# One scheduling block around a whole encoder kernel, ordered on another timing model

## Chip, cores and metric

The kernel runs on one core of one Trainium2 chip. The metric is the device time of one execution in microseconds (us); of several runs the median counts. Kernel before: median 1623.04 us of 3 runs, 1622.1 to 1624.04.

## What is computed

The reference is an encoder trunk of two layers over 512 tokens of width 1024, in float32:

```python
for layer in range(DEPTH):                       # 2
    h = rmsnorm(x, attn_norm[layer])
    proj = h @ w_in[layer]                       # 1024 x 6144: ten parts
    (a_q, a_k, a_v, b_q, b_ff, b_fb, b_i, b_g, gate_a, gate_b) = split_columns(proj)
    y_a = diff_attention(a_q, a_k, a_v, cos, sin, ...) @ w_a[layer]     # 4 heads, 2 softmaxes each
    y_b = hgrn2_bidirectional(b_q, b_ff, b_fb, b_i, b_g, ...) @ w_b[layer]   # 4 heads, gated recurrence
    merged = jax.nn.sigmoid(gate_a) * y_a + jax.nn.sigmoid(gate_b) * y_b
    x = x + merged @ w_o[layer]
    h = rmsnorm(x, ffn_norm[layer])
    x = x + (jax.nn.silu(h @ w_gate[layer]) * (h @ w_up[layer])) @ w_down[layer]   # hidden 2816
return rmsnorm(x, final_norm)
```

## The kernel before

**Arithmetic.** Every large product is made of three matmuls in a rounded float32 format: an operand is split into a high part (a cast on ScalarE) and a low part (a subtraction on VectorE), and `mm3` (line 207) multiplies high by high, high by low and low by high into the same PSUM bank. Activations are kept split in `hh` and `hl`, tokens along the free dimension; weights come as 1 MB loads into two buffers `raw` (`wload`, line 188, all on SyncE's DMA queue, SP) and are split into three buffers each of `hi` and `lo` (`wsplit`, line 196). `project_fm` (line 212) takes 128 output columns at a time: one split, 24 matmuls into one of four banks `m`, and a function that empties the bank. `project_tm` (line 234) does the same with tokens on the partitions.

**Stages of a layer.** First the projections that the recurrence needs. Then the recurrence, `hgrn_head` (line 412), head by head: a long chain of small steps on VectorE and ScalarE, with short groups of TensorE matmuls between them: transposes `kt` (line 494), states `st` (501), six groups of scores `sc` (548), `nr` (586 and 587), outputs `po` (599) and a norm `hss`. Beside them TensorE has projections for later steps to do. Then attention (line 627): sixteen steps, each with scores `qk` (662, 665), a softmax on VectorE and ScalarE, transposes `wt` (712), and for each head a product with the values; beside it the rest of the gate projections and w_b. Then w_a (its inputs are `oah` and `oal`), w_o, and the FFN (from line 828): one stream of matmuls through w_gate, w_up and w_down without small groups. The last layer ends in the final norm and the output.

**What sets the order.** The kernel is traced as one straight program. The Tile framework then decides the order of the instructions of each engine: it plays the program on a timing simulation of the chip, and each time an engine can take an instruction, it gives it the ready one of the highest priority. Priority is the place in the traced program; what is traced under `urgent()` (`tc.high_priority`) goes first of all: weight loads, splits, and the emptying of banks. So TensorE's order comes from three things: what the simulation takes for ready at a time, the place in the program, and edges added by hand. `behind(a, b)` (line 94) is such an edge: `a` is issued after `b`, without a wait on the chip; `tc.issue_after` is the same for a whole passage. Once the order is decided, each engine runs its own list strictly as it is listed, and semaphores hold an instruction until its operands are there. Pools with `reuse_waits="tile"` take over the memory of a pool before tile by tile. GpSimd makes an identity, five masks and constants at the start and does nothing later.

The change touches the place where the pools are opened, lines 100 to 105.

Of the kernel before, what the change touches and what calls it, by code (L numbers as in the profile page):

```python
# [47 lines left out]
def kernel(  # L48
# [45 lines left out]
    def behind(ins, other):  # L94
# [2 lines left out]
                          mybir.DependencyInfo(mybir.DependencyClass.NoSync, mybir.DependencyReason.DATA),  # L97
                          reason="keep the tensor engine from waiting")

    cp = ctx.enter_context(tc.tile_pool(name="const", bufs=1))  # L100
    wp = ctx.enter_context(tc.tile_pool(name="wraw", bufs=2))
    hp = ctx.enter_context(tc.tile_pool(name="wsplit", bufs=3))
# [862 lines left out]
```

## Time and profile before

| | |
|---|---|
| median of 3 runs | 1623.04 us |
| the profiled execution's own time | 1622.27 us |
| its span, first to last instruction | 1620.5 us |
| granted TensorE clock, mean | 0.999 of full |
| TensorE matmuls in the records | 7473 |
| VectorE, ScalarE busy in the span | 1013.2 us, 773.2 us |
| HBM read | 139.23 MB |

The profile is of one execution. Its page gives each engine's busy time; the windows give the same for stretches of the span, which show the stages: recurrence and attention of the first layer lie in the first 400 us, its FFN in the next 400, and the second layer repeats this in 800 to 1200 and 1200 to the end. A wait in the profile is idle time of an engine just before an instruction, with the instruction that released it. Matmuls are pipelined and the profile models their ends, so TensorE can be recorded as busy without working at its full pace; the number of matmuls in a stretch shows the pace. "PEld" is the loading of weights into TensorE, "SPq" SyncE's DMA queue.

### The profile page before, as it was taken

The page shows a single profiled execution, that of the slowest core. Times are in us where ns is not written, and L with a number is a line of the kernel's source. Part 1 is how long each engine was busy: PE and PEld are TensorE (multiplying, and loading weights), DVE is VectorE, ACT ScalarE, POOL GpSimd, SP SyncE. Part 2 cuts the span into 40 slices and gives each one's busy share as a digit, 9 for nine tenths or more (in the row PEclk, how much of TensorE's full clock was granted, in tenths as well). Part 3 has the DMA queues.
Part 4 walks back from the last instruction along what each step waited for, and adds up shares of the span by engine and source line. Part 5 has one row for each costly group of instructions (what it writes and reads, how often), then busy time and mean ns, then how long its engine had stood idle before and what let it go on. Part 6 is the DMA issues. An engine that isn't in the chain of part 4 may idle for free.

```text
span 1620.5 us, 18760 instructions
## 1 busy us (share of the span) xinstructions
PE 1604.7 (99%) x7473; PEld 1324.6 (82%) x7473; DVE 1013.2 (63%) x1637; ACT 773.2 (48%) x1188; POOL 8.5 (1%) x21
## 2 busy tenths in 40 slices
PE   9999999999999999999999999999999999999998
PEld 7888888887888888888888888888878888888886
DVE  8888977877654444433468789788875444444224
ACT  4666666676433323322355667676754323233213
POOL 2000000000000000000000000000000000000000
PEclk9999999999999999999999999999999999999999
DMA  6212221221333222322322222122123233332321
GB/s 203 91 57 73 79 68 63 79 78 52 105 104 98 85 88 94 115 90 99 103 89 87 70 79 78 54 77 79 52 79 98 84 104 104 105 101 94 104 82 74
DMA packets 118071, 142.53 MB, mean 88 GB/s; under 512 B 3168, under 2 KB 100704, under 8 KB 117984
## 3 DMA queue, kind: packets, MB, share of 16 engines
q1 hardware_dynamic: 117696, 141.05, 26.8%
q8 instruction: 58, 0.95, 0.2%
q10 hardware_dynamic: 288, 0.30, 0.1%
q14 instruction: 29, 0.24, 0.0%
HBM read 139.23 MB, written 2.10 MB: 87 GB/s over the span
## 4 chain that ended last, share of the span: by engine, by line
PE 86%; DVE 9%; ACT 3%; issue 1%; DMA 0%; SPq 0%; DVEq 0%; ACTq 0%
PE m L210 25%; PE m L208 24%; PE m L209 24%; DVE fl L81 2%; DVE lo L81 2%; PE sc L548 2%; PE s L209 1%; PE s L210 1%; PE s L208 1%; PE qk L665 1%; DVE z L81 1%; PE wt L712 1%; PE po L599 1%; PE qk L662 1%; ACT hi L92 1%
## 5 line engine op out<-in xcount | busy, mean ns | idle before, releaser
L92 ACT CAST hi<-raw 128x1024 fp32r<-128x1024 f32 (+2 forms) x274 | 272.2, 995 | 616.2 <-PE m L209 483.6
L208 PE MATMUL m<-hh,hi 128*128 128x512 f32 x1216 | 475.1, 391 | 0.7 <-ACT hh L78 0.7
L210 PE MATMUL m<-hh,lo 128*128 128x512 f32 x1216 | 475.3, 391 | 0.0
L209 PE MATMUL m<-hl,hi 128*128 128x512 f32 x1216 | 474.8, 391 | 0.0
L81 DVE TENSOR_TENSOR lo<-raw,hi 128x1024 fp32r<-128x1024 f32 (+2 forms) x282 | 321.0, 1139 | 181.6 <-ACT hi L92 180.2
L208 PEld LDWEIGHTS m<-hh,hi 128*128 128x128 f32 x1216 | 228.3, 188 | 48.5 <-ACT hh L78 1.9
L210 PEld LDWEIGHTS m<-hh,lo 128*128 128x128 f32 x1216 | 228.3, 188 | 47.3 <-DVE lo L81 0.6
L209 PEld LDWEIGHTS m<-hl,hi 128*128 128x128 f32 x1216 | 228.4, 188 | 46.9
L81 DVE TENSOR_TENSOR gu<-m,rbc 128x512 f32<-128x512 f32 x88 | 60.9, 692 | 241.6 <-PE m L210 237.6
L208 PE MATMUL m<-hi,hh 128*128 128x512 f32 x256 | 101.4, 396 | 0.0
L210 PE MATMUL m<-hi,hl 128*128 128x512 f32 x256 | 100.9, 394 | 0.0
L209 PE MATMUL m<-lo,hh 128*128 128x512 f32 x256 | 100.9, 394 | 0.0
L78 ACT ACTIVATE fl<-fl 128x1024 f32<-128x1024 f32 (+1 forms) x56 | 48.5, 872 | 43.6 <-DVE fl L81 43.5
L208 PE MATMUL m<-gh,hi 128*128 128x512 f32 x176 | 68.5, 389 | 0.0
L209 PE MATMUL m<-gl,hi 128*128 128x512 f32 x176 | 68.5, 389 | 0.0
L210 PE MATMUL m<-gh,lo 128*128 128x512 f32 x176 | 68.5, 389 | 0.0
L210 PEld LDWEIGHTS m<-hi,hl 128*128 128x128 f32 x256 | 48.1, 188 | 9.6
L208 PEld LDWEIGHTS m<-hi,hh 128*128 128x128 f32 x256 | 48.2, 188 | 9.3
L209 PEld LDWEIGHTS m<-lo,hh 128*128 128x128 f32 x256 | 48.2, 188 | 9.3
L548 PEld LDWEIGHTS sc<-fl 128*128 128x128 f32 x384 | 49.1, 191 | 7.0 <-issue 2.3
L548 PE MATMUL sc<-fl 128*128 128x128 f32 x384 | 51.3, 276 | 1.8 <-DVE fl L81 1.7
L209 PE MATMUL m<-ml,hi 128*128 128x512 f32 x128 | 49.7, 391 | 0.0
(258 smaller groups left out, 2349.9 us busy)
## 6 DMA issues: line engine op xcount, KB each, us to landing
raw<-in_w_in_dram SPq DMA_DIRECT2D x46, 1024.0 KB, 5.0
raw<-in_w_gate_dram SPq DMA_DIRECT2D x22, 1024.0 KB, 5.1
raw<-in_w_up_dram SPq DMA_DIRECT2D x22, 1024.0 KB, 5.2
raw<-in_w_down_dram SPq DMA_DIRECT2D x19, 1024.0 KB, 4.7
raw<-in_w_o_dram SPq DMA_DIRECT2D x8, 1024.0 KB, 4.8
raw<-in_w_b_dram SPq DMA_DIRECT2D x4, 1024.0 KB, 4.8
raw<-in_w_a_dram SPq DMA_DIRECT2D x4, 1024.0 KB, 5.0
raw<-in_w_down_dram SPq DMA_DIRECT2D x4, 768.0 KB, 4.1
```

Source lines behind the costliest of these rows:

```text
L78: return ACT.activation(o, i, func, **kw)
L81: return DVE.tensor_tensor(o, a, b, op)
L92: return ACT.copy(hi, src), tt(lo, src, hi.bitcast(F32), ALU.subtract)
L208: PE.matmul(ps, lh, rh, start=start, stop=False)
L209: PE.matmul(ps, lh, rl, start=False, stop=False)
L210: PE.matmul(ps, ll, rh, start=False, stop=stop)
L548: mm = PE.matmul(ps[:, c], K[:, c], Q[:, c], start=True, stop=True)
L599: mm = PE.matmul(po[:, tok], a, b, start=i == 0, stop=i == len(terms) - 1)
L662: mm = PE.matmul(ps[c], q2[:, c, tok], ka[:, c, :], start=True, stop=False)
L665: PE.matmul(ps[c], q2[:, c, tok], kb[:, c, :], start=False, stop=True)
L712: tr = PE.transpose(pt[:, s * P:(s + 1) * P], w[:, 0, s * P:(s + 1) * P], ident)
```

## The change

One line is added ahead of the pools, so that everything traced after it, which is the whole program, lies in one block:

```diff
+    ctx.enter_context(tc.block(schedule_with_timeline_sim=True))
     cp = ctx.enter_context(tc.tile_pool(name="const", bufs=1))
     wp = ctx.enter_context(tc.tile_pool(name="wraw", bufs=2))
     hp = ctx.enter_context(tc.tile_pool(name="wsplit", bufs=3))
```

`tc.block` traces its body into a basic block of its own, which is entered unconditionally and scheduled as a unit. With `schedule_with_timeline_sim=True` the framework orders that block on the second of its two timing simulations, which models the machine in more detail; the framework's own text names one thing that the first leaves out, a fixed cost of GpSimd's elementwise instructions. Everything else stays as it was: the traced instructions, their priorities, the edges added by hand, tiles, pools and buffer counts.

## The prediction

> **What bounds the kernel now.** I read the page first, then busy time by stage, then TensorE's waits, then its groups by shape.
>
> ```profile
> span 1620.5 us, 18760 instructions
> PE 1604.7 (99%) x7473; PEld 1324.6 (82%) x7473; DVE 1013.2 (63%) x1637; ACT 773.2 (48%) x1188; POOL 8.5 (1%) x21
> PE 86%; DVE 9%; ACT 3%; issue 1%; DMA 0%; SPq 0%; DVEq 0%; ACTq 0%
> ```
>
> TensorE (PE) is busy nearly throughout and makes up 86% of the chain that ended last. The windows show whether it is also fed at its own pace (columns: window, length, then busy time and count of PE, weight loads, VectorE, ScalarE, GpSimd, the clock, DMA):
>
> ```profile
> 0.00:50.00 50.00, 47.88 (x201) 38.10 (x202) 37.93 (x116) 27.51 (x38) 8.47 (x21) 1.00 0.52 175
> 50.00:100.00 50.00, 48.36 (x245) 40.25 (x244) 47.08 (x86) 27.88 (x43) 0.00 (x0) 1.00 0.26 84
> 150.00:200.00 50.00, 48.94 (x260) 41.08 (x259) 46.41 (x88) 29.76 (x53) 0.00 (x0) 1.00 0.26 85
> 350.00:400.00 50.00, 48.53 (x218) 38.23 (x217) 35.60 (x63) 32.17 (x60) 0.00 (x0) 1.00 0.13 43
> 600.00:650.00 50.00, 50.00 (x222) 41.39 (x221) 23.27 (x28) 14.79 (x18) 0.00 (x0) 1.00 0.28 86
> 950.00:1000.00 50.00, 49.37 (x257) 41.22 (x256) 48.92 (x89) 30.36 (x48) 0.00 (x0) 1.00 0.26 85
> 1150.00:1200.00 50.00, 48.55 (x219) 38.28 (x218) 35.66 (x64) 32.89 (x61) 0.00 (x0) 1.00 0.13 43
> sum 1650.00, PE 1604.71 PEld 1324.58 DVE 1013.20 ACT 773.18 POOL 8.47; mean PE 48.63 PEld 40.14 DVE 30.70 ACT 23.43 POOL 0.26
> ```
>
> Window 600 to 650 lies in the FFN: 222 matmuls of 512 columns in 50 us, no idle, 225.2 ns each. That is PE's pace when fed. The other six windows lie in the start, in the recurrence and at the two ends of attention, and there PE is idle for 2.1 + 1.6 + 1.1 + 1.5 + 0.6 + 1.5 = 8.4 us. The waits of PE name the same places (us in total, times, longest):
>
> ```profile
> PE m L210 <- DVE lo L81: 1.8, 2, 0.9
> PE sc L548 <- DVE fl L81: 1.7, 3, 1.1
> PE idle L266 <- DVE ones_r L119: 1.4, 1, 1.4
> PE st L501 <- ACT kt L496: 1.2, 1, 1.2
> PE m L208 <- ACT oah L92: 1.2, 2, 0.6
> PE m L208 <- ACT hh L78: 0.7, 1, 0.7
> PE nr L587 <- DVE kl L81: 0.3, 1, 0.3
> PE kt L494 <- ACT fs L78: 0.2, 1, 0.2
> PE qk L665 <- DVE kb L81: 0.2, 1, 0.2
> ```
>
> They sum to 8.7 us, 1.4 of it the very start. The records can hide more, since a matmul's end is modelled. So I count the work itself, by PE's groups (last columns: busy us and mean ns, then the idle before them):
>
> ```profile
> L548 PE MATMUL sc<-fl 128*128 128x128 f32 x384 | 51.3, 276 | 1.8 <-DVE fl L81 1.7
> L665 PE MATMUL qk<-kb,q 128*128 128x512 f32 x64 | 26.0, 406 | 0.5 <-DVE kb L81 0.2
> L712 PE MATMUL wt<-ident,e 128*128 128x128 f32 x128 | 19.2, 273 | 0.0
> L599 PE MATMUL po<-fs,S 128*128 128x128 f32 x96 | 15.9, 275 | 0.0
> L599 PE MATMUL po<-A,vB 128*128 128x128 f32 x64 | 12.5, 277 | 0.0
> L501 PE MATMUL st<-vB,kt 128*128 128x128 f32 x96 | 12.4, 279 | 1.2 <-ACT kt L496 1.2
> L494 PE MATMUL kt<-ident,fs 128*128 128x128 f32 x48 | 7.0, 275 | 0.2 <-ACT fs L78 0.2
> L638 PE MATMUL qkt<-ident,ak 128*128 128x128 f32 x32 | 4.8, 273 | 0.0
> L638 PE MATMUL qkt<-ident,aq 128*128 128x128 f32 x32 | 4.8, 272 | 0.0
> L884 PE MATMUL xt<-ident,xT 128*128 128x128 f32 x32 | 3.9, 276 | 0.1
> L210 PE MATMUL m<-oah,lo 128*128 128x512 f32 x64 | 24.6, 394 | 1.8 <-DVE lo L81 1.8
> L208 PE MATMUL m<-oah,hi 128*128 128x512 f32 x64 | 24.6, 394 | 1.2 <-ACT oah L92 1.2
> ```
>
> ```profile
> 227.58 2.02 PE po L599 x18
> 1487.50 2.53 issue
> ```
>
> Of the narrow ones, 384 + 128 + 96 + 64 + 96 + 48 + 3 x 32 = 912 have 128 columns, and eighteen of them in a row take 2.02 us, 112 ns each. So 912 x 0.112 + 6561 x 0.2252 = 102.1 + 1477.5 = 1579.7 us of matmuls, if nothing ever waited. The end lies behind them:
>
> ```profile
> 1613.78 0.28 PE L210 MATMUL s<-hi,gl 128*128 128x256 f32 x1
> 1616.99 0.35 ACTq L927 DMA_DIRECT2D out_dram<-xt  x1
> ```
>
> 1620.5 - 1614.1 = 6.4 us of tail and 1.4 us of start stand outside. What order could still give back inside is at most 1620.5 - 1579.7 - 6.4 - 1.4 = 33 us, of which 7.3 show as waits.
>
> [...] The page shows the weight loads busy for 82% of the span. [...]
>
> **The change part by part.** No arithmetic, operand, transfer or tile is added or removed. Three things change.
>
> *Which order each engine's instructions get.* Where PE has one stream of work only, there is nothing to reorder: I cost the FFN windows at 0, covered by the packed row 600 to 650. Where recurrence or attention is mixed with projections, PE switches between project_fm's matmuls (24 to a tile of 128 columns, 24 x 0.2252 = 5.4 us) and small groups that wait for VectorE or ScalarE. Those groups, from the rows above (records by records in one group): sc 384 / 8 = 48, st 96 / 6 = 16, kt 48 / 3 = 16, qk 64 / 2 = 32, wt 128 / 4 = 32, po 8 (one a head), 152 in all. Today the waits name 3 + 1 + 1 + 1 = 6 of them (sc, st, kt, qk), 3.3 us, 0.55 us a wait. The other 146 arrive after their operands. A new order is made from times of a model; how well they fit, no row shows. Bounds: below, all waits inside go and as much again of the hidden loss (-15 us); above, all 152 wait 0.55 us (+84 - 3 = +80). I take the value by the place. A late operand can't be made up where VectorE has no idle time: it is busy 47.1, 46.4 and 48.9 of 50 us in three windows, and at the two ends of attention, PE already waits for w_a's operands with the filler matmuls used up. That is five of the sixteen windows of 50 us in 0 to 400 and 800 to 1200, so 152 x 5 / 16 = 48 groups, x 0.55 = 26 us, less the 3.3 there now: **+23 us**.
>
> *What else moves with it.* The weight splits are traced at top priority and stay early in any order, but their exact place decides when the raw buffers come free:
>
> ```profile
> L81 DVE TENSOR_TENSOR lo<-raw,hi 128x1024 fp32r<-128x1024 f32 (+2 forms) x282 | 321.0, 1139 | 181.6 <-ACT hi L92 180.2
> SPq L193 <- DVE lo L81: 1432.3, 123, 38.3
> raw<-in_w_gate_dram SPq DMA_DIRECT2D x22, 1024.0 KB, 5.1
> ```
>
> SP's queue always waits for that split, then a load lands in 5.1 us and feeds 48 matmuls, 10.8 us. A split 1.1 us later moves the load by 1.1 us inside 5.7 us of cover: 0, and in FFN the same. If the cover went, the 123 waiting loads would each show what is over.
>
> *The block itself.* Each engine enters and leaves a block of instructions of its own. No row shows such a branch. Bounds: 0 (a fall-through; a gain is excluded, nothing is left out for it), and for one stall the longest time on the chain in which an engine waited for nothing that the profile shows, 2.53 us at 1487.5, where ScalarE reloads its table. Once at each end makes 5.1 us. I take 0, since the first loads come from SP at once in the same program, and keep 5 for the range.
>
> [...]
>
> The profiled execution took 1622.27 us, its span and 1.8 us around it; 1622.3 + 23 = 1645. The median of the runs is 0.8 us higher than that execution, so I round to 1646 us.
>
> **The rivals.**
>
> *The new order fits better (faster).* The model counts what the first one leaves out, so each small group is placed where its operands have landed. For it: the 6 waits of the small groups are such misfits, and projections stand ready to fill them. Against it: 33 us is all there is, and the 1.8 + 1.2 = 3.0 us before w_a's matmuls (rows m<-oah) at the attention ends have no filler. Time: 1622.3 less 7.3 - 3.0 = 4.3 shown and the same to twice that of hidden loss, -9 to -13: 1609 to 1614, I say 1612. It decides if fewer than those 6 groups wait.
>
> *Engines are filled ahead (much slower).* If the model lets PE take several ready matmuls before a small group becomes ready, every hand-off queues behind half a projection tile, 2.7 us. Attention makes 32 qk and 32 wt hand-offs, in series within a head: 64 x 2.7 = 173 us of longer chain, hidden as long as projections are left to run. They are used up by the end of attention today (rows m<-oah, windows 350 to 400 and 1150 to 1200), so part shows; a quarter to a half, 43 to 86 us: 1665 to 1708, I say 1685. For it: PE at 99% shows that it nearly always has other work ready. Against it: the manual edges (behind) hold some projections back.
>
> *Nothing moves that matters.* The order comes out nearly the same, because priorities, manual edges and buffer counts leave little choice, or since the models differ mainly for GpSimd, which works 8.47 us, all in the first window. 1623, within 3. Against it: 152 groups are placed by time.
>
> **How the numbers follow.** Forecast (small misfits) 0.31, its own range 1628 to 1665; filled ahead 0.23; fits better 0.28; no difference 0.18. A difference under 0.2% (3.2 us) is about what a measurement here can't tell from none. Slower: 0.31 + 0.23 = 0.54; same 0.18; faster 0.28. The range: below 1609 lies some 0.07 of the better-fit case, above 1692 about 0.11 of filled ahead, so 1609 to 1692.
>
> **What would show it.** Right: the count of each group unchanged, FFN windows still 222 matmuls in 50 us, PE idle grown in the windows with VectorE above 46 us and at the ends of attention, with sc, st, qk and oah named in PE's waits at about 0.5 us each and a few dozen times. Filled ahead: projections of gates finished early, then long stretches in attention with PE well under 48 of 50. Fits better: PE's waits inside under 4 us. Wrong altogether: a loss inside FFN, at the first load, or a grown tail.

## The result and the profile after

The changed kernel takes 1764.64 us (median of 4 runs, 1763.42 to 1766.52). The kernel before takes 1622.57 us (4 runs, 1622.08 to 1624.04). The ratio is 1.0876, its 95% interval 1.0864 to 1.0889: 142 us slower. The forecast was 1646 us with a range up to 1692. Its sign held; its size did not, and neither did the mechanism that it took for the likeliest.

The profiled execution after took 1766.52 us. From its page: span, engines, the chain that ended last, and TensorE's busy share and granted clock in 40 slices of 44 us.

```profile
span 1764.8 us, 18744 instructions
PE 1652.9 (94%) x7473; PEld 1362.2 (77%) x7473; DVE 1022.1 (58%) x1637; ACT 775.7 (44%) x1188; POOL 8.6 (0%) x21
PE 88%; DVE 7%; ACT 4%; issue 1%; DVEq 0%; ACTq 0%
PE   9998896996899999999999987879968999999998
PEclk9998996998899999999999999989989999999999
```

The work is the same, 7473 matmuls, but the span is 144 us longer, and the slices under 9 lie in two stretches, slices 4 to 11 and 24 to 31: the recurrence and attention of the two layers (slice 40 holds the tail). The windows of the kernel after, with the columns as in the prediction, say when inside them:

```profile
50.00:100.00 50.00, 50.00 (x243) 42.06 (x242) 40.20 (x72) 26.56 (x42) 0.00 (x0) 1.00 0.32 105
100.00:150.00 50.00, 50.00 (x257) 42.44 (x256) 38.60 (x65) 25.82 (x38) 0.00 (x0) 1.00 0.23 74
150.00:200.00 50.00, 38.79 (x179) 32.91 (x178) 37.14 (x73) 25.55 (x42) 0.00 (x0) 0.80 0.03 12
250.00:300.00 50.00, 33.29 (x145) 27.60 (x143) 28.28 (x57) 19.31 (x32) 0.00 (x0) 0.69 0.07 21
400.00:450.00 50.00, 33.68 (x129) 22.24 (x127) 36.88 (x72) 27.72 (x62) 0.00 (x0) 0.86 0.00 0
600.00:650.00 50.00, 50.00 (x223) 41.40 (x222) 22.90 (x28) 14.71 (x18) 0.00 (x0) 1.00 0.27 85
```

Read the first two rows beside the third. From 50 to 100 us TensorE is fuller than it was before (50.00 of 50 where 48.36 stood), while VectorE does less (40.20 where 47.08 stood) and the weight loads run ahead (105 GB/s where 84 stood). It stays full to 150 us. Then TensorE stands still: 11.2 us in 150 to 200, 16.7 us in 250 to 300, 16.3 us in 400 to 450, and hardly any weights are loaded there (DMA share 0.03, 0.07 and 0.00). What TensorE gained early it did not have later. The FFN row, 223 matmuls in 50 us, is as before (222).

The waits of TensorE after, the first rows (us in total, times, longest):

```profile
PE sc L549 <- DVE fl L81: 25.0, 11, 3.7
PE m L209 <- DVE avl L84: 13.6, 2, 6.8
PE m L209 <- ACT oah L92: 11.7, 6, 2.9
PE hss L405 <- ACT sqh L398: 11.6, 9, 1.3
PE m L209 <- DVE sg L81: 8.1, 2, 6.9
```

All such rows together sum to 105 us, against 8.7 before: 96 us more. The other 48 us of the longer span are in TensorE's busy time (1652.9 against 1604.7 for the same matmuls). Part of that is the clock, shown further down.

**Where it starts.** The first head of the recurrence, from the timelines (start, length, instruction, count, idle time before it). Before:

```profile
77.09 1.06 PE L548 MATMUL sc<-fl 128*128 128x128 f32 x8
...
80.74 1.06 PE L548 MATMUL sc<-fl 128*128 128x128 f32 x8
...
83.94 1.06 PE L548 MATMUL sc<-fl 128*128 128x128 f32 x8
...
88.04 1.06 PE L548 MATMUL sc<-fl 128*128 128x128 f32 x8
```

After:

```profile
79.68 1.06 PE L549 MATMUL sc<-fl 128*128 128x128 f32 x8
...
86.73 1.05 PE L549 MATMUL sc<-fl 128*128 128x128 f32 x8
...
93.55 1.05 PE L549 MATMUL sc<-fl 128*128 128x128 f32 x8
...
101.50 1.06 PE L549 MATMUL sc<-fl 128*128 128x128 f32 x8
```

The same groups came 3.65, 3.20 and 4.10 us apart and now come 7.05, 6.82 and 7.95 us apart, and TensorE does not idle between them. The timelines say what lies between the six groups: 12, 10, 14, 14 and 5 matmuls of projections before, 27, 26, 31, 29 and 19 after. For the first three gaps that is 15, 16 and 17 more; at 0.2265 us, the spacing of projections in these timelines, 3.40, 3.62 and 3.85 us. The gaps grew by 3.40, 3.62 and 3.85 us. So the whole stretching of these gaps is projections put ahead of a group that has to wait for them in TensorE's list. VectorE's timeline after shows that the groups' operands were there:

```profile
84.39 0.69 DVE L81 TENSOR_TENSOR fl<-fl,q 128x512 f32<-128x512 f32 x1
87.82 0.42 DVE L81 TENSOR_TENSOR fl<-cum 128x256 f32<-128x256 f32 x1 [2.74 <-PE sc L549]
...
90.38 0.69 DVE L81 TENSOR_TENSOR fl<-fl,q 128x512 f32<-128x512 f32 x1
```

The first row ends the operand `fl` of the group at 93.55, 8.5 us ahead of it, the last row that of the group at 101.50, 10.4 us ahead; before, the same two groups came 0.7 and 1.6 us after theirs. The middle row shows how the delay is handed on: VectorE starts the next `fl` only when the group at 86.73 has released a buffer.

How far this carries: the norm `hss` closes a head. The tile's rows, first and last start of the four heads, before (layer 1's recurrence, then attention in layers 1 and 2):

```profile
L404 PE MATMUL hss<-sqh,ones_r x4: 404/404/404, 107.4 to 233.3; 128*128 128x512 f32 x4
...
L407 PE MATMUL hss<-sql,ones_r x4: 389/402/424, 299.9 to 384.9; 128*128 128x512 f32 x4
...
L407 PE MATMUL hss<-sql,ones_r x4: 389/398/431, 1100.8 to 1185.8; 128*128 128x512 f32 x4
```

and after:

```profile
L405 PE MATMUL hss<-sqh,ones_r x4: 398/451/499, 140.4 to 285.4; 128*128 128x512 f32 x4
...
L408 PE MATMUL hss<-sql,ones_r x4: 389/398/503, 375.4 to 455.3; 128*128 128x512 f32 x4
...
L408 PE MATMUL hss<-sql,ones_r x4: 389/398/503, 1248.9 to 1329.3; 128*128 128x512 f32 x4
```

In layer 1 the first head of the recurrence ends 33 us later, the fourth 52 us later, attention 70 us later. When attention of layer 2 ends, 143.5 us are lost, nearly all of the 144 us of the longer span: 73 us of it in layer 2. About three quarters of layer 1's 70 us were there at the end of the recurrence.

### The profile page after: what moved, and what is told of

Same layout as the page of the kernel before. It is cut to its first block, busy times and chain, and to the rows that moved or that the text cites. A ratio compares the mean times of both kernels' runs of the same rounds, so it can differ in the third digit from the quotient of the medians.

```text
span 1764.8 us, 18744 instructions
## 1 busy us (share of the span) xinstructions
PE 1652.9 (94%) x7473; PEld 1362.2 (77%) x7473; DVE 1022.1 (58%) x1637; ACT 775.7 (44%) x1188; POOL 8.6 (0%) x21
## 4 chain that ended last, share of the span: by engine, by line
PE 88%; DVE 7%; ACT 4%; issue 1%; DVEq 0%; ACTq 0%
PE m L209 26%; PE m L210 26%; PE m L211 25%; PE sc L549 2%; DVE fl L81 2%; PE s L211 1%; PE s L210 1%; PE s L209 1%; PE po L600 1%; ACT hsq L78 1%; ACT fl L78 1%; ACT e L78 1%; PE qk L666 1%; PE qk L663 1%; PE wt L713 0%
## 5 line engine op out<-in xcount | busy, mean ns | idle before, releaser
L549 PE MATMUL sc<-fl 128*128 128x128 f32 x384 | 61.6, 314 | 25.7 <-DVE fl L81 25.0
L549 PEld LDWEIGHTS sc<-fl 128*128 128x128 f32 x384 | 57.3, 223 | 30.8 <-DVE fl L81 17.1
L211 PEld LDWEIGHTS m<-hi,hl 128*128 128x128 f32 x256 | 49.2, 192 | 10.4
L78 ACT ACTIVATE e<-qk,nm 128x512 f32<-128x512 f32 x64 | 43.8, 687 | 18.9 <-DVE nm L668 18.8
```

Source lines behind the costliest of these rows:

```text
L78: return ACT.activation(o, i, func, **kw)
L211: PE.matmul(ps, ll, rh, start=False, stop=stop)
L549: mm = PE.matmul(ps[:, c], K[:, c], Q[:, c], start=True, stop=True)
```

## The experiments

Three theories were stated. The first (T1): the second simulation lets TensorE take instructions well ahead of the time at which they run, so a group that becomes ready lands behind projections already taken; projections are used up early, and the chain then runs with nothing beside it. The second (T2): the same, but on VectorE and ScalarE. The third (T3): it is the times of the second model that put groups in wrong places. A rival without any order is the block itself. The second simulation has a setting for each engine, how many instructions it may hold ahead while the order is made; the kernel after has the simulation's own, 35 for TensorE and 12 for VectorE and ScalarE. They are settings of a model: how many instructions the chip's engines hold ahead, no trace here shows. The kernels below change that setting; the chip, the work and the edges stay. In the cuts of code each statement has a line of its own, and "..." marks what is left out. The runs of the kernel before that stand beside the experiments have a median of 1622.26 us.

**The block without the second simulation** (block_only).

```diff
-    ctx.enter_context(tc.block(schedule_with_timeline_sim=True))
+    ctx.enter_context(tc.block())
```

> The block stays, the second simulation goes (tc.block() without the argument). If the order from the second simulation is the cause, this runs as the kernel before: 1619 to 1627 us. If it is the block (its entry and exit, or that it is scheduled as a unit), it stays near 1765.

Measured: 1622.05 us, ratio 0.9998 (0.9989 to 1.0008). Its span was 1620.4 us at a mean granted clock of 0.999, against 1620.5 us and 0.999 before. The block costs nothing that can be measured; the loss is the order.

**TensorE two ahead** (pe_ahead_2): the change, with 2 in place of 35 for TensorE.

```diff
+from concourse.hw_specs import TRN2Spec
+TRN2Spec.ENG_ISSUE_QUEUE_DEPTH[mybir.EngineType.PE] = 2
```

> The changed kernel with one parameter of the second simulation changed: PE may take 2 instructions ahead of the one it works on, not 35. Theory 1, PE filled ahead (each small group queues behind about 35 x 0.226 = 8 us of projections): the projections between two sc groups fall from 26-31 to 11-17 and the time to 1615 to 1650. Theory 2, VectorE and ScalarE filled ahead (12 each, unchanged here): over 1730. Theory 3, the finer times of the model themselves place the groups badly: over 1730.

Measured: 1627.43 us, ratio 1.0032 (1.0021 to 1.0043). 137 of the 142 us are gone with this one number. The times of the second model are the same in this kernel, so T3 falls as the main cause. Windows of this kernel:

```profile
150.00:200.00 50.00, 50.00 (x265) 42.74 (x264) 46.19 (x92) 28.85 (x51) 0.00 (x0) 1.00 0.26 85
...
350.00:400.00 50.00, 44.67 (x192) 35.50 (x191) 34.36 (x62) 28.99 (x56) 0.00 (x0) 0.93 0.12 42
```

The recurrence is full again, fuller than before (50.00 where 48.94 stood). What is left to lose lies mostly at the end of attention, where its waits name w_a's operands, as before but longer, and `hss`; the one wait of 2.2 us for `avl` lies earlier in layer 2:

```profile
PE m L209 <- ACT oah L92: 5.7, 2, 2.9
PE hss L405 <- ACT sqh L398: 2.7, 2, 1.3
PE m L209 <- DVE avl L84: 2.2, 1, 2.2
```

**VectorE and ScalarE one ahead, TensorE at 35** (dve_act_ahead_1).

```diff
+TRN2Spec.ENG_ISSUE_QUEUE_DEPTH.update({mybir.EngineType.DVE: 1, mybir.EngineType.Activation: 1})
```

> The counterpart: PE stays at 35 ahead, VectorE and ScalarE may take 1 instead of 12. Theory 1: 1750 to 1775, the same long pauses in recurrence and attention. Theory 2: 1615 to 1660. Theory 3: 1750 to 1775 as well; only the run with PE at 2 parts it from theory 1.

Measured: 1758.37 us (one run); 27, 28, 26, 29 and 19 projections between the first head's groups, and a window that stands nearly as it does in the kernel after:

```profile
250.00:300.00 50.00, 33.77 (x147) 27.97 (x146) 29.13 (x59) 20.62 (x35) 0.00 (x0) 0.69 0.06 21
```

T2 falls as the cause. **Both small** (all_ahead_small: TensorE 2, VectorE and ScalarE 1):

> Both: PE 2, VectorE and ScalarE 1. Theory 1: as the run with PE at 2 alone, within 15 us. Theory 2: this one alone, or together with the run with VectorE and ScalarE at 1, is fast. Theory 3: over 1730.

Measured: 1628.59 us, ratio 1.0038 (1.0023 to 1.0053), no better than TensorE's alone.

**The two orders of TensorE crossed.** A function at the end of the kernel takes TensorE's matmuls in traced order and adds edges that hold them to a stored list, without a wait on the chip:

```diff
+def pin(tc):
+    pe = [i for i in tc.nc.cur_bb.bb.instructions
+          if i.engine == mybir.EngineType.PE and type(i).__name__ == "InstMatmult"]
...
+    for a, b in zip(order, order[1:]):
+        tc.add_manual_dep(pe[b], pe[a].name,
+                          mybir.DependencyInfo(mybir.DependencyClass.NoSync, mybir.DependencyReason.DATA),
+                          reason="order of another schedule")
```

pe_order_of_before is the changed kernel with TensorE's list of before:

> The changed kernel, with TensorE's own list of matmuls pinned, by edges of issue order alone, to the list of the kernel before; VectorE, ScalarE and SP are still ordered on the second simulation. If TensorE's order alone makes the loss (theory 1 in its strict form): 1615 to 1640. If the orders of the other engines carry a part of the 142 us, that part stays: over 1660.

pe_order_of_after is the kernel before, without a block, with TensorE's list of after:

> The kernel before, no block, with TensorE's list pinned to that of the changed kernel; the other engines are ordered on the first simulation around it. Theory 1 in its strict form: 1745 to 1785, though neither the block nor the second simulation is there. If TensorE's order is only a follower of the others: under 1680.

Measured: 1633.4 us, ratio 1.0071 (1.0054 to 1.0088), and 1756.56 us (one run). The four corners:

| TensorE's list | other engines ordered by the first simulation | by the second |
|---|---|---|
| of before | 1622.3 | 1633.4 |
| of after | 1756.6 | 1764.6 |

TensorE's list alone costs 134 us down the one column and 131 down the other; the simulation that orders all other engines 11 and 8. (Their lists were made anew around the pinned one, so a column does not repeat them instruction for instruction.) The waits of pe_order_of_after, made by the first simulation for every other engine, are much like those of the kernel after:

```profile
PE sc L548 <- DVE fl L81: 25.1, 12, 3.7
PE hss L404 <- ACT sqh L397: 11.0, 9, 1.3
PE m L208 <- DVE avl L84: 10.3, 2, 5.1
```

and those of pe_order_of_before are small groups whose operands come late:

```profile
PE sc L549 <- DVE fl L81: 5.2, 7, 1.7
PE kt L495 <- ACT fs L78: 3.2, 1, 3.2
```

So T1's place, TensorE's list, is shown from both sides. Which of the other engines makes the 8 to 11 us was not tried.

**The dose.** TensorE 4, 12 and 20 ahead, to see whether the loss grows with the number:

> The second simulation with TensorE at 4 ahead. The straight line gives 1627 + 2 x 4.4 = 1636. If what is left at 2 (5 us over the kernel before) has nothing to do with the number ahead, 4 is as good as 2: 1624 to 1630.

> The second simulation with TensorE at 12 ahead. 12 x 0.226 = 2.7 us at each small group against 7.9 at 35 and 0.5 at 2. Theory 1: in between, 1630 to 1690, with 17 to 20 projections between sc groups, and the pauses shorter than at 35.

> The second simulation with TensorE at 20 ahead. So far 2 gave 1627, 12 gave 1671, 35 gave 1765: (1671 - 1627) / 10 = 4.4 and (1765 - 1671) / 23 = 4.1 us for each instruction more. Theory 1 as a straight line: 1671 + 8 x 4.1 = 1704, range 1690 to 1720. If the loss comes all at once, where projections run out in one stage more: near 1671 or near 1765.

| TensorE ahead | projections between the first head's groups | us |
|---|---|---|
| kernel before | 12, 10, 14, 14, 5 | 1622.3 |
| 2 | 12, 11, 11, 14, 5 | 1627.4 |
| 4 | 12, 11, 11, 14, 5 | 1631.45 (ratio 1.0058, 1.0042 to 1.0073) |
| 12 | 17, 18, 20, 17, 8 | 1671.19 (one run) |
| 20 | 20, 19, 19, 25, 12 | 1713.09 (one run) |
| 35 (the change) | 27, 26, 31, 29, 19 | 1764.6 |

The time rises by 4.4 us an instruction from 2 to 12, 5.2 from 12 to 20 and 3.4 from 20 to 35: no step, but a fairly steady price for each instruction taken ahead. 20 came out in its expected range; 4 lies between its two expectations; there the first head's counts are those of 2, and its 4 us more show in one wait, that for `avl` (6.0 us where 2 ahead has 2.2). The counts of one head are a sign and not the price: all_ahead_small has 18, 17, 11, 14 and 4 there, near those of 12 ahead, and takes 1628.59 us.

**One ahead** (pe_ahead_1): the other end.

> The second simulation with TensorE at 1 ahead: its TensorE then hardly overlaps anything, and only 4 or 5 projections stand between two sc groups. The other side of the same theory: now the groups come too early, their operands aren't there, TensorE waits at sc for VectorE's fl many times, 1 to 2.5 us each. 40 sc groups x 2 us = 80 us: 1680 to 1760. If fewer projections ahead were simply better, it would be under 1627.

Measured: 1941.62 us (one run), worse than the change. The direction was foreseen; the time lies 180 us above the expected range. The list holds 4, 4, 4, 5 and 1 projections between the groups. Its waits:

```profile
PE sc L549 <- DVE fl L81: 44.1, 31, 2.4
PE m L209 <- DVE q L81: 33.7, 4, 15.3
PE qk L666 <- DVE kb L81: 17.1, 16, 2.2
```

and its first window of the recurrence:

```profile
50.00:100.00 50.00, 34.13 (x134) 27.38 (x135) 28.43 (x47) 15.71 (x23) 0.00 (x0) 0.76 0.24 77
```

Groups now come too early and TensorE waits for them, and the projections listed behind wait with it. In the first head the group at 107.56 us has waited 1.05 us for `fl`, and the projection behind it starts at 108.48 with no wait of its own: the list is kept in this direction too. All its rows of idle time sum to 217 us, spread over the recurrence, attention and the edges of stages; why the order is so bad with one instruction ahead is settled by none of these runs. The steady price above holds from 2 to 35 and not below.

**Filler for the end of attention.** The 5 us left at 2 ahead show mostly as waits before w_a. Here the last tile of gate_a's projection (24 matmuls, 5.4 us) is held back behind `tr`, the last transpose of attention, first with TensorE 2 ahead (held_ahead_2), then in the kernel before (held_first_sim):

```diff
-                    mm3(ps, wh[:, c, :], wl[:, c, :], ah[:, c, :], al[:, c, :], c == 0, c == k - 1)
+                    mm = mm3(ps, wh[:, c, :], wl[:, c, :], ah[:, c, :], al[:, c, :], c == 0, c == k - 1)
+                    c == 0 and i + j in hold and behind(mm, hold[i + j])
...
-                        project_fm(win, [G_A + (4 * j + i) * P for i in range(4)], scaled(lambda i: ga[j][:, i, :]))
+                        project_fm(win, [G_A + (4 * j + i) * P for i in range(4)], scaled(lambda i: ga[j][:, i, :]),
+                                   hold={i: tr for i in range(4) if 4 * j + i >= 7})
```

> TensorE at 2 ahead, and the last column tile of the gate projection (24 matmuls, 5.4 us) held by an edge behind the last transpose of attention in both layers, so that it stands between the last small groups. At 2, TensorE loses 9 us at each end of attention, 7 of it in the waits ao, hss and oah. If those are waits for want of a projection to do: 5 us less in each layer, 1617, under the kernel before. If the projection is then missing earlier in attention, nothing is gained: 1622 to 1632.

> The kernel before with the same edge and no block. It loses about 3 us at each end of attention. If the projection held back fills that and is not missed earlier: 1616 to 1619; if it is missed earlier: 1621 to 1630.

Measured: 1629.14 us, ratio 1.0040 (1.0027 to 1.0054), and 1632.1 us, ratio 1.0061 (1.0048 to 1.0074): no gain in the one, 10 us lost in the other. The waits of held_ahead_2 no longer name `oah` first, but the transposes `wt` just ahead of it:

```profile
PE wt L713 <- DVE e L84: 7.0, 3, 4.0
PE wt L713 <- DVE den L673: 3.9, 1, 3.9
```

and those of held_first_sim likewise:

```profile
PE wt L712 <- ACT e L78: 7.5, 2, 3.8
```

The tile fills the pause it is moved to and is missed where it was. At this place filler looks short, not misplaced; other tiles and other places were not tried. No version tried here beats the kernel before; the nearest with the second simulation is TensorE 2 ahead, 0.3% slower.

## Why the prediction was wrong

**What bounds the kernel.** Right: TensorE near its pace, 33 us at most to give back (35, since 18 of the 6561 matmuls priced at 0.2252 us have 256 columns and start 0.12 us apart). No order tried gave any of it back. That the list matters this much in the other direction follows from the same row: an engine that is 99% busy has no slack to catch up with.

**The likeliest case** is the step that failed. It took the second simulation for a model with somewhat other times, priced a misplaced group at 0.55 us, the mean of the six waits before, and counted 48 of them in places where VectorE has no idle time or filler is used up: +23 us where 142 were measured. After, TensorE idles 96 us more, `sc` alone 11 times for 2.3 us each. More to the point, the loss does not start with groups whose operands are late: in the first head TensorE never idles, the operands lie ready, and the group lies behind 27 projections. Late operands come afterwards, when the stretched chain has no projections left beside it. The mean of today's waits could not show that price, since today's list holds no such place.

**Filled ahead**, given 0.23 and 1685 us, is what happened, and the dose shows its mechanism. Its size failed in two terms. The hand-off was priced at half a projection tile, 2.7 us; measured are 15 to 17 more projections, 3.4 to 3.9 us. And the sum counted attention's 64 hand-offs, a quarter to a half of them showing, and left out the recurrence with its `sc`, `st` and `po` groups. There lie 52 of the first layer's 70 us. Its reason "hidden as long as projections are left to run" was right, but their end was put at the end of attention, as it is before; after, they run out for the first time in the second head (152 us). The two first heads alone, 33 us in layer 1 and 29 us in layer 2 (`hss` at 907.2 us before and 1006.4 after, less the 70 us of layer 1), would have put 62 us into that sum before attention was counted.

What spoke against this case, that the manual edges hold some projections back, was a misreading of the kernel: on TensorE `behind` and `issue_after` stand on small groups (such as scores, states, transposes and norms, or the first head as a whole) and on no projection, so they could only put the small groups later.

**Fits better** and **nothing moves** are out: the windows of the recurrence and of attention changed, and the fuller early windows were paid for later. A fixed cost of GpSimd's instructions, which the first simulation was said to leave out, shows in no row: GpSimd is busy 8.63 us in the first window after, 8.47 before.

**The terms at nothing.** The block at 0 is right (1622.05 against 1622.26 us), and FFN at 0 is right (223 matmuls in 50 us). No trace shows whether the block adds a branch to an engine's instructions; whatever it adds, block_only puts its price inside 0.9989 to 1.0008, that is under 2 us. The loads at 0 cannot be told alone: they land as fast as before (a load for w_gate in 5.1 us in both pages), yet they run ahead and then stop with the projections, as the windows' last column shows.

**What it said it would see.** The list for "filled ahead" was met nearly in its words: projections finished early, then stretches with TensorE well under 48 of 50. Only it named attention, and the first such stretch is at 150 us.

## What to carry to other kernels

When an order is made by playing a model, ask first how far ahead the model lets an engine commit, before asking how good its times are: on an engine that keeps to its list, as TensorE did here, each instruction taken ahead of a waiting group is a delay of the chain (15 to 17 more projections, 3.40 to 3.85 us a gap in the first head), and it costs even when the engine never idles, because it uses up the filler that a later part of the chain needs (here from 152 us on). Less is not always better: here 2 ahead gave 1627 us, 35 ahead 1765 us and 1 ahead 1942 us. Read a schedule by what lies between two dependent small groups (here 12 projections or 27) and by whether busy windows early are followed by empty ones later. One window that gets fuller is no gain if the work it took was the cover of the next.

## What the runs showed of the chip that was not expected

After the longer pauses TensorE itself was slower for some microseconds. The timeline after, at the point where the projections run out:

```profile
152.47 1.95 PE L549 MATMUL sc<-fl 128*128 128x128 f32 x16
157.99 2.08 PE L549 MATMUL sc<-fl 128*128 128x128 f32 x8 [3.58 <-DVE fl L81]
161.15 2.07 PE L549 MATMUL sc<-fl 128*128 128x128 f32 x8 [1.08 <-DVE fl L81]
164.99 2.07 PE L549 MATMUL sc<-fl 128*128 128x128 f32 x8 [1.77 <-DVE fl L81]
...
167.72 0.63 PE L211 MATMUL m<-hi,hl 128*128 128x512 f32 x1
168.15 0.63 PE L209 MATMUL m<-hi,hh 128*128 128x512 f32 x1
...
171.62 0.39 PE L209 MATMUL m<-hi,hh 128*128 128x512 f32 x1
171.84 0.39 PE L210 MATMUL m<-lo,hh 128*128 128x512 f32 x1
```

After an idle time of 3.58 us, eight narrow matmuls take 2.08 us where 1.06 was usual, and when the projections come back they start 0.43 us apart, not 0.22, until 171 us, some 4.5 us after the stream is dense again. After the pauses of 6.82, 6.89 and 6.82 us that end at 293.49, 1071.85 and 1166.65 us the projections start 0.43 us apart as well; after one of 1.74 us, at 405.59, the matmuls behind it start 0.23 us apart. The windows' clock column shows the same, 0.80 and 0.69 where full windows have 1.00, and the mean over the span is 0.963 where 0.999 stood. So the chain left alone cost twice here, once by its waits and once by the speed of its own groups, 2.08 us for eight matmuls. How much of the 142 us this is can only be bounded: in the timeline 77 matmuls of 512 columns start 0.40 to 0.46 us before the next with no wait between them, 5 in the kernel before, 72 x 0.2 = 14 us; what the narrow groups lost to the clock lies somewhere in the other 34 us of grown busy time and was not separated.
